# The first layer's experts in tiles of 32 columns, with a fixed order on the tensor engine and one block of whole-array matmuls per pair of experts

## The chip, the cores and the metric

The kernel runs on one core of a Trainium2 chip, all in fp32. The metric is the time of one execution on the device in microseconds (us), as the median of the runs shown. TensorE is PE below, its weight loads PEld, VectorE DVE, ScalarE ACT, GpSimd POOL and the queue that starts the loads SP.

## The reference, cut to what matters

The program computes a two-layer block (a state-space mixer, then experts; attention, then experts) on 512 rows of 1024 features and a context of 256 rows, and then a second block. The change lies in the experts of the first layer, which run twice: for the 512 rows of `x` (64 rows an expert) and for the 256 rows of the context (32 rows an expert). The 16 experts' weights are the same for both sets.

```python
N_EXPERTS, EC_CAPACITY, D_EXPERT = 16, 2, 1024
def moe_ec(h, router_w, w1, w3, w2):
    ...
    cap = EC_CAPACITY * T // N_EXPERTS          # 64 for x, 32 for the context
    aff = jax.nn.softmax(logits, axis=-1)
    gate, idx = lax.top_k(jnp.swapaxes(aff, 1, 2), cap)
    xg = h[bidx, idx]
    a = jnp.einsum('becd,edf->becf', xg, w1)
    g = jnp.einsum('becd,edf->becf', xg, w3)
    y = jnp.einsum('becf,efd->becd', jax.nn.silu(a) * g, w2)
    y = y * gate[..., None].astype(y.dtype)
    return jnp.zeros_like(h).at[bidx, idx].add(y.astype(h.dtype))
...
x = x + g2l * moe_ec(rmsnorm(x, norm2_w[i]) * (1.0 + sc2l) + sh2l, ...)
ctx = ctx + g2c * moe_ec(rmsnorm(ctx, norm2_w[i]) * (1.0 + sc2c) + sh2c, ...)
```

## The kernel before, in words

`Kern.moe` (L1073) goes over eight pairs of experts. For each pair there are three products, with w1, w3 (both in `moe_up`, L1151) and w2 (in `moe_down`, L1196). Here the gathered rows are the stationary operand (the weights of the array, in PE's sense) and the experts' weight matrices stream through as the moving one, 512 columns at a time. A product has eight K tiles of 128 features, so the stage has 8 pairs x 3 products x 8 = 192 K tiles. `moe_product` (L1132) issues for each K tile:

- the big set (L1142): for each half of the columns and each of the two experts a matmul whose stationary operand has 64 columns (the expert's 64 rows); the two experts take columns 0 to 63 and 64 to 127 of the array by `tile_position=(0, 64 * e)`. Results are `pa`, `pg` or `py`.
- the small set (L1148): for each expert and each half a matmul with 32 stationary columns; the four take the four quarters of the array's columns. Results are `ca`, `cg` or `cy`.

An fp32 matmul of this kind is two passes on PE, each with its own load, so the profile lists 8 passes of the big set and 8 of the small one for each K tile. The word **step** below means one pass of all tiles that share the array's columns: two passes side by side for tiles of 64 columns, four for tiles of 32.

The weights come through `Ring` (L106): nine tiles of 1 MiB, each two K tiles of one expert, loaded by SP (L125, L130) as the places come free. Around the products stand matmuls that use the whole array: `Router.quad` (L328) gathers the rows of four experts by a product with one-hot matrices (L343, 64 passes for each quad, results `xxg`; evicted by ACT at L347 and DVE at L349), `gates` (L351) does 16 small ones (L360), `flip` in `moe_up` transposes the activations (L1179, results `aT` and `cT`, evicted by ACT and DVE), and `moe_down` puts the results back: `scaled` multiplies by the gate and splits into `yhi` and `ylo` (L1226 ACT, L1227 DVE), `slots` makes one-hots `ohT` from a small matmul `sp` (L1233, L1237 DVE), and `scatter` multiplies the two (L1244, L1245, result `sc`) and adds it to the residual in SBUF (L1246, DVE; `xT` is the big set's residual, the `cT` with 128x256 elements the small one's). `after` (L1063) puts the gates of the first quad after pair 0's products with w1 and w3, and a gather with its gates after those of pairs 1, 3 and 5.

Nobody writes down the order of the engines: a scheduler merges the program's parts, by what is ready, into one list for each engine. PSUM is dealt out by `Slots` (L93), a table of banks by tag; the tags of this stage are `a`, `g`, `c` and `x`, two banks each.

Of the kernel before, what the change touches and what calls it, by code (L numbers as in the profile page):

```python
# [13 lines left out]
F32 = mybir.dt.float32  # L14
F32R = mybir.dt.float32r
# [7 lines left out]
P = 128  # L23
D = 1024
KT = 8
# [7 lines left out]
# columns of the packed per-feature vectors: (name, number of 128-tiles)  # L33
# [14 lines left out]
class SumSq:  # L48
    """Squares of [128, n] tiles summed tile by tile; the last ones stay apart until the sum over partitions."""
# [43 lines left out]
class Slots:  # L93
    """all of PSUM, bank by bank; the banks of a tag take turns"""
    MAP = dict(mm=(0, 1, 2), ada=(3,), aux=(4, 5), y=(6, 7), a=(0, 1), g=(2, 3), c=(4, 5), x=(6, 7), am=(0, 1, 4, 5), rms=(2, 3), vps=(6, 7))
# [39 lines left out]
class Head:  # L135
    """the second block's beginning: its h, as the residual becomes final, and the first products' part of the features that come early"""
# [25 lines left out]
    def begin(self, wp, pp):  # L162
        """products of the first four K tiles"""
# [22 lines left out]
class Pre:  # L186
    """hi + lo = x * gain of tokens a..b, with the sums of squares of x; 1/rms comes in at the end of the products."""
# [21 lines left out]
class Router:  # L209
    """Expert choice of the rows h = x * rs * A + sh of one set of tokens; residual tiles are fed as they become final."""  # L210

    def __init__(self, K, layer, xp, res, n, cap, c, nm):
# [28 lines left out]
    def score(self, k):  # L241
        """tile k's part of the logits and of the squares"""
# [19 lines left out]
    def turn(self, q):  # L262
        """tiles 4q..4q+3, times 1/rms, as rows"""
# [11 lines left out]
    def finish(self):  # L275
# [30 lines left out]
        # the cap largest of every expert (equal ones: the first), numbered from 1 by their place; 0: not taken  # L306
# [21 lines left out]
    def quad(self, q, pp, *tags):  # L328
        """gathered rows of 256 slots, transposed: xg[d, (expert, slot)]"""
# [21 lines left out]
    def gates(self, q, pp, tag):  # L351
        """the gates of the rows of the last quad"""
        K, nc, nt, cap, ne, oh = self.K, self.K.nc, self.nt, self.cap, self.ne, self.oh
        # gates: all experts' affinities of every slot, then the slot's own
# [6 lines left out]
        if cap == 32:  # L361
            # every row twice: for the two halves of the products' rows
# [15 lines left out]
class Kern:  # L378
# [24 lines left out]
    def consts(self):  # L403
# [18 lines left out]
        # silu of the conditioning, padded to a 32-column stationary operand  # L422
# [15 lines left out]
    def split(self, pool, raw, n=1024, eng=None):  # L438
        """raw (f32) = hi + lo, both exact in float32r."""
# [7 lines left out]
    def jobs(self, wp, jobs, look=1):  # L447
        """jobs: (weights or None, work). Weights are made ready some jobs ahead of their work; the background goes on after each product."""
# [28 lines left out]
    def dense(self, wp, pp, srcs, nk, act, rngs, evac, tag="mm", cols=P):  # L477
        """out^T tiles: srcs[i] holds [128, nk*cols] (pieces of <=1024 columns) of one tile of cols columns."""
# [24 lines left out]
    def rms(self, tp, pp, tiles, n, dim, tag="aux", rs=None, eng=None):  # L503
        """1/sqrt(mean of squares + eps) of the features in tiles (list of [128, n]), on all partitions."""
# [5 lines left out]
    def rs_of(self, tp, ps, n, dim, rs=None, after=None):  # L510
        """1/sqrt(ps / dim + eps); after: the activation that the table set for it may follow"""
# [8 lines left out]
    def table(self, after):  # L520
        """loads the table set that has both Ln and Exp; what is in the context comes after that"""
# [7 lines left out]
    # ------------------------------------------------------------------ modulation  # L529
# [4 lines left out]
    def ada_steps(self, tp, pp, layer, grp, tag, ttag="aux"):  # L534
        """one third of a layer's modulation, K tile by K tile"""
# [24 lines left out]
    def ada_half(self, tp, pp, hf):  # L560
        """shift and scale before the first mixer, of one half of the features"""
# [28 lines left out]
    def modulated(self, tp, src, rs, n, A, sh, hi, lo, f32=None, ks=range(KT)):  # L590
        """h = src * rs * A + sh, split to hi + lo (and kept whole in f32 if asked)."""
# [11 lines left out]
    # ------------------------------------------------------------------ layer 0: SSD mixer  # L603
    def ssd(self, e0, esc, rest):
        """The whole mixer of layer 0. e0: lives until the layer's end; esc: holds the context's residual; rest(cT): opens what follows,
        gives xT and the routers."""
# [5 lines left out]
        with ExitStack() as so:  # L612
# [6 lines left out]
            # triangles: tle[s, l] = s <= l, tge[s, l] = s >= l  # L619
# [40 lines left out]
            # the last scans run beside the context's output projection  # L660
# [23 lines left out]
            # fills the tensor engine's time until the choice is made  # L684
# [11 lines left out]
    def ssd_dt(self, tp, wp, pp, h, K, aS):  # L696
        """time steps, their running sums in each chunk (forward and backward heads) and decays"""
# [3 lines left out]
        # work in tiles of the first group, which come later  # L701
# [44 lines left out]
    def log1p(self, u, w, m, l):  # L746
        """u <- log(1 + u), accurate for small u (u >= 0)."""
# [11 lines left out]
    def ssd_in(self, g, wp, gp, pp, h, K, between):  # L759
        """convolved B, C, x and the gate 2*silu(z) of a group; tokens: latent, then context"""  # L760
# [7 lines left out]
        if g == 0:  # L768
            # as h comes
# [48 lines left out]
    def ssd_group(self, g, gp, pp, K, conv, zs):  # L818
        """the scans of a group, in twelve steps for the tensor engine to take between projections"""
# [36 lines left out]
        def prepare(c):  # L856
# [4 lines left out]
            # the smaller one of the two directions' exponents is the one that applies: forward for l > s, backward for l < s, 0 for l = s  # L861
# [102 lines left out]
    def ssd_proj(self, tp, yp, wp, pp, a, b, res, c, eng):  # L964
        """residual += gate * (gated norm of y) @ out_w for tokens a..b; yields after every K tile (None) and final tile (its number)"""
# [6 lines left out]
        for hf in range(2 // per):  # L972
# [33 lines left out]
            # the last two K tiles bank by bank, so that the banks get free one after the other  # L1006
# [28 lines left out]
        # slot number (from 1) of a partition: p % 64 + 1; for the halved set p % 32 + 1 in one half of every 64, none in the other  # L1035
# [12 lines left out]
        # fold[32 j + e, e'] = (e == e')  # L1048
# [3 lines left out]
        # twice[32 e + j, 64 e + 32 h + j] = 1  # L1052
# [10 lines left out]
    def after(self, r, pr, pp):  # L1063
        """what comes after the first products of a pair"""
# [8 lines left out]
    def moe(self, st, layer, R, nw2):  # L1073
        """R: routers of the sets (the first one with 64 slots an expert, the second one with 32)"""
# [1278 lines left out]
```

## Time and profile before

| | us |
|---|---|
| median of three runs | 3469.9 (3468.0 to 3475.1) |
| span of the profiled execution | 3464.9 |
| busy in the span: PE / PEld / DVE / ACT / POOL | 3278.8 / 2045.4 / 1667.4 / 1139.2 / 926.2 |
| the first layer's experts, from the end of the first quad's gather to the end of the last product | 941.8 to 1660.4 |
| from there to the first matmul of attention's projections | 1660.4 to 1679.9 |

The profile is one execution; the median of the runs lies 5.0 us above its span, and a predicted time below is a predicted span plus that. A busy share is time with any instruction in work. Matmuls overlap in the records, so what a step takes is read from the distance between the starts of records and not from their lengths. In a timeline a row can stand for several records ("x8"), with the start of the first; "128*64 128x512" is 128 rows by 64 stationary columns, moving operand 128x512.

### The profile page before, as it was taken

How to read it: one execution, taken by the hardware profiler on the slowest of the kernel's cores; microseconds unless marked ns; L12 is line 12 of the kernel's file. 1: busy time of each engine (PE TensorE's matmuls, PEld its weight loads, DVE VectorE, ACT ScalarE, POOL GpSimd, SP SyncE). 2: the span in 40 equal slices, each digit the busy share in tenths (PEclk: the TensorE clock that was granted, in tenths of full speed). 3: DMA queues.
4: the chain of work that ended last, by engine and by line, in shares of the span. 5: the costliest groups of instructions: out<-in, count | busy, mean ns of one | idle time of the engine just before them, and what ended most of it. 6: DMA issues, size and time to landing. Idle time of an engine off the chain costs nothing.

```text
span 3464.9 us, 44645 instructions
## 1 busy us (share of the span) xinstructions
PE 3278.8 (95%) x17408; PEld 2045.4 (59%) x17408; DVE 1667.4 (48%) x3070; ACT 1139.2 (33%) x2007; POOL 926.2 (27%) x638
## 2 busy tenths in 40 slices
PE   7999999989999999999899989998998999999998
PEld 4677777777623232322566754432356777888886
DVE  5588888886411111211456531003349954773322
ACT  4344444455300000000556520000135344573222
POOL 1344555543100000000341120000135454126543
PEclk9999999999999999999999999999999999999999
DMA  6454433454487767687234269999861322543232
GB/s 242 140 163 156 131 90 100 133 165 150 165 311 267 292 245 297 238 305 262 92 125 137 90 262 405 409 409 362 323 234 49 98 74 84 181 140 116 97 95 82
DMA packets 254083, 668.40 MB, mean 193 GB/s; under 512 B 19312, under 2 KB 73456, under 8 KB 252848
## 3 DMA queue, kind: packets, MB, share of 16 engines
q1 hardware_dynamic: 243920, 645.42, 52.1%
q10 hardware_dynamic: 9952, 20.12, 1.7%
q8 instruction: 137, 2.24, 0.3%
q14 instruction: 74, 0.61, 0.1%
HBM read 651.65 MB, written 13.83 MB: 192 GB/s over the span
## 4 chain that ended last, share of the span: by engine, by line
PE 60%; DVE 7%; DMA 4%; ACT 2%; issue 2%; POOL 1%; SPq 0%; DVEq 0%; POOLq 0%; ACTq 0%
PE pa L1142 7%; PE mm L473 6%; PE mm L475 6%; PE mm L474 6%; PE pg L1142 5%; PE py L1142 4%; PE py L1220 3%; DMA wm<-in_moe_w_dram 3%; PE ca L1148 2%; PE cg L1148 2%; PE gth L343 2%; PE cy L1148 2%; PE sc L1244 1%; PE pv L1436 1%; PE ptp L1427 1%
## 5 line engine op out<-in xcount | busy, mean ns | idle before, releaser
L444 POOL TENSOR_TENSOR wlo<-raw,whi 128x1024 fp32r<-128x1024 f32 (+3 forms) x207 | 461.4, 2231 | 1372.9 <-ACT whi L443 1339.4
L443 ACT CAST whi<-raw 128x1024 fp32r<-128x1024 f32 (+2 forms) x291 | 285.8, 984 | 486.6 <-PE mm L474 207.7
L473 PE MATMUL mm<-stk,whi 128*128 128x512 f32 (+2 forms) x944 | 342.8, 363 | 0.5 <-DVE pt__23035 L1581 0.5
L475 PE MATMUL mm<-stk,wlo 128*128 128x512 f32 (+2 forms) x944 | 336.1, 356 | 0.0
L474 PE MATMUL mm<-stk,whi 128*128 128x512 f32 (+2 forms) x944 | 335.4, 355 | 0.0
L1174 DVE TENSOR_TENSOR ac<-ac,pg 128x512 f32<-128x512 f32 x32 | 22.0, 687 | 531.5 <-PE pg L1142 531.0
L473 PE MATMUL pin<-hhi,whi 128*128 128x256 f32 (+1 forms) x768 | 271.5, 354 | 3.8 <-DVE acc L811 3.8
L475 PE MATMUL pin<-hhi,wlo 128*128 128x256 f32 (+1 forms) x768 | 265.5, 346 | 0.0
L474 PE MATMUL pin<-hlo,whi 128*128 128x256 f32 (+1 forms) x768 | 263.3, 343 | 0.0
L1142 PE MATMUL pa<-wm,xxg 128*64 128x512 f32 x760 | 223.6, 603 | 3.3 <-DMA wm<-in_moe_w_dram 2.8
L1142 PE MATMUL pg<-wm,xxg 128*64 128x512 f32 x712 | 209.4, 601 | 5.1 <-DMA wm<-in_moe_w_dram 5.1
L473 PEld LDWEIGHTS mm<-stk,whi 128*128 128x128 f32 (+1 forms) x944 | 180.3, 191 | 32.9 <-issue 7.9
L474 PEld LDWEIGHTS mm<-stk,whi 128*128 128x128 f32 (+1 forms) x944 | 180.0, 191 | 29.7 <-issue 5.9
L475 PEld LDWEIGHTS mm<-stk,wlo 128*128 128x128 f32 (+1 forms) x944 | 179.3, 190 | 25.9 <-issue 1.1
L58 POOL TENSOR_TENSOR sqa<-sqa,sq 128x256 f32<-128x256 f32 (+1 forms) x56 | 64.2, 1146 | 466.5 <-DVE acc L204 410.0
L473 PEld LDWEIGHTS pin<-hhi,whi 128*128 128x128 f32 x768 | 146.4, 191 | 45.0 <-issue 19.2
L474 PEld LDWEIGHTS pin<-hlo,whi 128*128 128x128 f32 x768 | 146.7, 191 | 19.6 <-DVE hlo L600 2.5
L475 PEld LDWEIGHTS pin<-hhi,wlo 128*128 128x128 f32 x768 | 146.4, 191 | 18.4 <-issue 1.7
L811 DVE SCALAR_TENSOR_TENSOR acc<-pin,cwh,acc 128x511 f32<-128x511 f32 (+3 forms) x256 | 148.5, 608 | 15.2 <-ACT acc L806 13.6
L1227 DVE SCALAR_TENSOR_TENSOR ylo<-py,xgate,yhi 128x512 fp32r<-128x512 f32 x32 | 24.0, 750 | 244.1 <-ACT yhi L1226 243.3
L1173 ACT ACTIVATE ac<-pa 128x512 f32<-128x512 f32 x32 | 19.0, 597 | 344.7 <-PE pa L1142 344.7
L1142 PEld LDWEIGHTS pg<-wm,xxg 128*64 128x64 f32 x712 | 59.1, 136 | 122.5 <-issue 95.4
(684 smaller groups left out, 7040.2 us busy)
## 6 DMA issues: line engine op xcount, KB each, us to landing
wm<-in_moe_w_dram SPq DMA_DIRECT2D x255, 1024.0 KB, 7.5
raw<-in_moe_w_dram SPq DMA_DIRECT2D x258, 512.0 KB, 6.9
raw<-in_ada_w_dram SPq DMA_DIRECT2D x96, 512.0 KB, 4.7
raw<-in_w_f_dram SPq DMA_DIRECT2D x68, 512.0 KB, 3.5
raw<-in_w_ssd_in_dram SPq DMA_DIRECT2D x48, 512.0 KB, 4.7
ab<-aS SPq DMA_DIRECT2D x96, 256.0 KB, 4.7
raw<-in_w_in_dram SPq DMA_DIRECT2D x33, 512.0 KB, 3.5
raw<-in_w_ssd_out_dram SPq DMA_DIRECT2D x32, 512.0 KB, 4.0
```

The costliest lines, as they stand in the source:

```text
L58: self.eng.tensor_tensor(self.acc, self.acc, self.late.popleft(), op=ALU.add)
L343: nc.tensor.matmul(ps[:, z2, :], r[:, t, k * P:(k + 1) * P], oh[:, t, :], start=(t == 0 and z == 0), stop=(t == nt - 1 and z == 1))
L443: nc.scalar.copy(hi[:, 0:n], raw[:, 0:n])
L444: (eng or self.lo).tensor_tensor(lo[:, 0:n], raw[:, 0:n], hi[:, 0:n].bitcast(F32), op=ALU.subtract)
L473: nc.tensor.matmul(ps, wh, ah, start=start, stop=False)
L474: nc.tensor.matmul(ps, wh, al, start=False, stop=False)
L475: nc.tensor.matmul(ps, wl, ah, start=False, stop=stop)
L811: nc.vector.scalar_tensor_tensor(o, p_[:, lo + s:hi + s], tap(j), o, op0=ALU.mult, op1=ALU.add)
L1142: nc.tensor.matmul(pb[hf][64 * e:64 * e + 64, :], lb(k, e), w[e][a][:, hf * 512:(hf + 1) * 512], tile_position=(0, 64 * e), **f)
L1148: nc.tensor.matmul(pc[o:o + 32, :], ls(k, e), w[e][a][:, hf * 512:(hf + 1) * 512], tile_position=(0, o), **f)
L1220: nc.tensor.matmul(py[half][64 * e:64 * e + 64, :], yb(k, e), w[e][a], start=(k == 0), stop=(k == KT - 1), tile_position=(0, 64 * e))
L1244: nc.tensor.matmul(ps[:, 0:n], y[0][:, kk * P:(kk + 1) * P], o, start=True, stop=False)
```

## The change

The first layer's `moe` no longer calls `moe_up` and `moe_down`. It has its own code (the second layer's `moe_last` keeps the old one), inside a block in which PE's order is the written one; the other engines are still scheduled.

```diff
-            after = self.after(R[0], pr, pp)
-            acts = self.moe_up(layer, pr, R, ring, ep, pp, after)
-            self.moe_down(layer, pr, R, ring, ep, pp, acts)
+        def product(nm, pr, lb, ls, pb, pc):
+            for q in range(4):
+                w = [ring.tile(...) for e in range(2)]
+                steps = [(a, z) for a in range(2) for z in (0, 1, 2)] if q < 3 else [(a, z) for z in (0, 1, 2) for a in range(2)]
+                for a, z in steps:
...
+                    for e in range(2):
+                        for h in range(2):
+                            o = 64 * e + 32 * h
+                            if z < 2:
+                                nc.tensor.matmul(pb[z][o:o + 32, :], lb(k, e)[:, 32 * h:32 * h + 32], w[e][a][:, z * 512:(z + 1) * 512], tile_position=(0, o), **f)
+                            else:
+                                nc.tensor.matmul(pc[o:o + 32, :], ls(k, e), w[e][a][:, h * 512:(h + 1) * 512], tile_position=(0, o), **f)
...
+        def scatter_small(y, o, k, kk):
+            ps = bank("scs", "s")
+            for j in range(2):
+                for z in range(2):
+                    nc.tensor.matmul(ps[:, j * C:(j + 1) * C], y[z][:, (kk + j) * P:(kk + j + 1) * P], o, start=j == 0 and z == 0, stop=j == 1 and z == 1)
+            for j in range(2):
+                t = ep.tile([P, C], F32, name="scc", tag="scc", bufs=2)
+                nc.scalar.activation(t, ps[:, j * C:(j + 1) * C], AF.Copy, scale=self.mod(layer, 5, 1, k + j))
+                nc.gpsimd.tensor_tensor(small.res[:, k + j, :], small.res[:, k + j, :], t, op=ALU.add)
...
+        with tc.manual_schedule(engines={mybir.EngineType.PE}):
+            big.quad(0, pp, "x", "c")
+            big.gates(0, pp, "x")
+            last = None
+            for pr in range(8):
+                product("moe_w1", ...)
+                ac = [silu(t) for t in (*pa, ca)]
+                product("moe_w3", ...)
+                for t, g in zip(ac, (*pg, cg)):
+                    nc.vector.tensor_tensor(t, t, g, op=ALU.mult)
+                for t, o in zip(ac, (aT[:, 0:4, :], aT[:, 4:8, :], cT)):
+                    flip(t, o)
+                if pr % 2 and pr < 7:
+                    big.quad(pr // 2 + 1, pp, "s")
+                    big.gates(pr // 2 + 1, pp, "s")
+                if last:
+                    scatter(*last)
+                product("moe_w2", ...)
+                last = (pr, [scaled(t, big.gate[:, pr:pr + 1]) for t in py], scaled(cy, small.gate[:, pr:pr + 1]))
+            scatter(*last)
```

In words:

- **Tiles.** The big set's matmul of 64 stationary columns becomes two of 32 (new L1101), so all products, the small set's (new L1103) too, go in quads of 32 columns. A K tile now has 16 passes of the big set and 8 of the small one, still six steps.
- **Order.** In the last quarter of each product the two K tiles of `pb[0]` come first, then those of `pb[1]`, then those of `pc`. All matmuls that use the whole array stand in one block for each pair, between the products with w3 and w2: 12 transposes, then for pairs 1, 3 and 5 a gather with its gates, then the scatter of the pair before (40 or so passes: `sp` twice, 16 `sc`, 16 `scs`). The last pair's scatter stands at the end. The gates of the first quad move ahead of pair 0.
- **Engines.** The big set's residual is still updated by DVE (new L1139). The small set's goes by a copy with scale on ACT (new L1148, `scc`) and an add on POOL (new L1149); before, both were DVE's.
- **Buffers.** A tag `s` of four PSUM banks (6, 0, 7, 1) serves the scatters and the later gathers; `ac`, `yhi` and `ylo` get a third buffer; the small one-hots get their own tag `ohS`. The silu of `pa` and `ca` is written ahead of the product with w3.

PE where pair 0's products end and pair 1's begin, in the kernel before (`sel` is a table for the one-hots, `xslotT` the slot numbers):

```order
L1142 MATMUL py<-wm,aT 64x512 x4
L1148 MATMUL cy<-wm,cT 32x512 x4
L1233 LDWEIGHTS sel
L1233 MATMUL sp<-xslotT,sel 128x512
L1142 MATMUL pa<-raw,xxg 64x512 x3
L1244 MATMUL sc<-ohT,yhi 128x512
L1245 MATMUL sc<-ohT,ylo 128x512
L1244 MATMUL sc<-ohT,yhi 128x512
L1245 MATMUL sc<-ohT,ylo 128x512
L1142 MATMUL pa<-raw,xxg 64x512
L1148 MATMUL ca<-raw,cxg 32x512
```

The scatter of pair 0 is spread in small pieces over the next pair's product with w1.

PE at the block of pair 2 in the changed kernel, from the end of the product with w3 to the start of that with w2 (`ident` is the identity matrix of the transposes, `ohS` the small set's one-hots):

```order
L1103 MATMUL cg<-raw,cxg 32x512 x2
L1103 MATMUL cg<-wm,cxg 32x512 x2
L1113 MATMUL tp<-ident,ac 128x128 x12
L1127 LDWEIGHTS sel
L1127 MATMUL sp<-xslotT,sel 128x512
L1127 LDWEIGHTS sel
L1127 MATMUL sp<-cslotT,sel 128x256
L1138 MATMUL sc<-ohT,yhi 128x512
...
L1145 MATMUL scs<-ohS,yhi 128x256
...
L1101 MATMUL py<-wm,aT 32x512 x8
L1103 MATMUL cy<-wm,cT 32x512 x4
```

No product matmul stands between the transposes and the last scatter any more; in the places marked "..." the sixteen `sc` and sixteen `scs` matmuls of pair 1 alternate, four and four.

POOL at the end of the stage, the difference (`wlo` is the low part of attention's weights, `kB` a buffer of attention that is cleared, `slots` the router's):

```order
 L325 TENSOR_TENSOR slots<-slots,wk 16x512
 L326 CAST xslotT<-slots 16x512
-L444 TENSOR_TENSOR wlo<-raw,whi 128x1024 x3
-L1311 MEMSET kB 64x3072
+L1149 TENSOR_TENSOR cT<-cT,scc 128x256 x56
+L444 TENSOR_TENSOR wlo<-raw,whi 128x1024 x2
+L1411 MEMSET kB 64x3072
+L1149 TENSOR_TENSOR cT<-cT,scc 128x256 x2
+L444 TENSOR_TENSOR wlo<-raw,whi 128x1024
+L1149 TENSOR_TENSOR cT<-cT,scc 128x256 x6
```

POOL had no work of this stage; it now has 64 adds, and the last eight stand behind two splits and the clearing, with a third split between them.

## Rows read from the trace of the kernel before

**Rows 1.** By stretch: span, busy PE to POOL, PE clock, DMA share, GB/s.
```profile
941.80:1660.40 718.60, 715.31 (x3664) 208.02 (x3662) 128.45 (x236) 46.05 (x85) 0.00 (x0) 1.00 0.74 278
994.50:997.90 3.40, 3.40 (x9) 0.95 (x6) 1.85 (x5) 0.35 (x2) 0.00 (x0) 0.51 1.02 419
1660.40:1679.90 19.50, 17.64 (x63) 9.95 (x59) 13.55 (x25) 13.27 (x21) 10.74 (x11) 0.91 0.25 84
2100.00:2300.00 200.00, 194.61 (x944) 86.17 (x941) 21.09 (x46) 16.36 (x32) 0.00 (x0) 1.00 1.03 409
```

**Rows 2.** Timeline, one K tile: start, length, engine, line, names, shapes, records.
```profile
965.44 1.94 PE L1142 MATMUL pa<-raw,xxg 128*64 128x512 f32 x8
967.31 1.07 PE L1148 MATMUL ca<-raw,cxg 128*32 128x512 f32 x8
968.30 0.64 PE L1142 MATMUL pg<-raw,xxg 128*64 128x512 f32 x1
```

**Rows 3.** Timeline, PE: four quads of 32 columns, two lone passes, what follows.
```profile
63.55 2.76 PE L542 MATMUL ada<-raw,sc 128*32 128x512 f32 x18
66.25 0.38 PE L473 MATMUL pin<-hhi,whi 128*128 128x256 f32 x1
```

**Rows 4.** Timeline, PE: pair 0's scatter between pair 1's first matmuls.
```profile
1020.73 1.93 PE L1142 MATMUL pa<-raw,xxg 128*64 128x512 f32 x6
1022.59 0.50 PE L1244 MATMUL sc<-ohT,yhi 128*128 128x512 f32 x1
...
1023.16 0.40 PE L1244 MATMUL sc<-ohT,yhi 128*128 128x512 f32 x1
1023.39 0.40 PE L1245 MATMUL sc<-ohT,ylo 128*128 128x512 f32 x1
1023.72 1.07 PE L1142 MATMUL pa<-raw,xxg 128*64 128x512 f32 x2
```

**Rows 5.** Timeline, PE: short passes of the scan, transposes, gathers.
```profile
731.53 0.61 PE L900 MATMUL y<-ce,hst 128*64 128x128 f32 x8
731.97 0.39 PE L900 MATMUL y<-w,rowx 128*64 128x128 f32 x4
...
993.02 1.28 PE L1179 MATMUL tp<-ident,ac 128*128 128x128 f32 x8
...
1085.75 0.28 PE L343 MATMUL gth<-xoh,xrh 128*128 128x256 f32 x1
1085.86 0.28 PE L343 MATMUL gth<-xoh,xrl 128*128 128x256 f32 x1
```

**Rows 6.** Groups by line and form, 930 to 1670: busy us, mean ns, idle before.
```profile
L1174 DVE TENSOR_TENSOR ac<-ac,cg 128x512 f32<-128x512 f32 x8 | 5.5, 684 | 0.4
L1181 DVE COPY aT<-tp 128x256 f32<-128x256 f32 x16 | 6.7, 421 | 5.5 <-ACT aT L1180 5.5
L1237 DVE TENSOR_SCALAR ohT<-sp,iop 128x512 fp32r<-128x512 f32 x8 | 5.9, 742 | 0.0
L1237 DVE TENSOR_SCALAR ohT<-sp,iop 128x256 fp32r<-128x256 f32 x14 | 6.1, 475 | 0.0
L1246 DVE SCALAR_TENSOR_TENSOR xT<-sc,mods,xT 128x512 f32<-128x512 f32 x63 | 45.2, 747 | 51.8 <-PE sc L1245 51.7
```

**Rows 7.** Groups, timeline, and the chain's last two lines: the stage's end.
```profile
L58 POOL TENSOR_TENSOR sqa<-sqa,sq 128x256 f32<-128x256 f32 x36 | 34.5, 957 | 27.1 <-ACT sq L65 26.4
...
1661.64 7.05 POOL L444 TENSOR_TENSOR wlo<-raw,whi 128x1024 fp32r<-128x1024 f32 x3 [739.90 <-ACT whi L443]
1672.43 2.66 POOL L1311 MEMSET kB<- 64x3072 f32 x1 [3.74 <-DVE ohT L1237]
...
L1266 ACT ACTIVATE sq<-xT 128x512 f32<-128x512 f32 x8 | 5.0, 631 | 4.6 <-PE rmsps L1268 4.6
...
1675.89 0.87 PE rmsps L1268 x2
...
1679.89 0.96 PE mm L473 x3
```

More of the change, by code (lines that the diff above doesn't have):

```diff
@@ L1073, in moe @@
     def moe(self, st, layer, R, nw2):
+        nc, tc = self.nc, self.tc
         ep = self.pool(st, "moe_e")
-        R[0].xgp = ep
+        big, small = R
+        big.xgp = ep
         rings, _ = self.wm1[:-1], self.wm1[-1]
         if nw2:
-            rings.append((st.enter_context(self.tc.tile_pool(name="moe_w2", bufs=nw2, side="right")), nw2))
+            rings.append((st.enter_context(tc.tile_pool(name="moe_w2", bufs=nw2, side="right")), nw2))
         ring = Ring(self, rings, 3)
-        pp = self.pp or self.pool(st, "moe_ps", bufs=2, space=PSUM)
@@ L1082, in moe @@
-        R[0].quad(0, pp, "x", "c")
-        for pr in range(8):
-            after = self.after(R[0], pr, pp)
-            acts = self.moe_up(layer, pr, R, ring, ep, pp, after)
-            self.moe_down(layer, pr, R, ring, ep, pp, acts)
+        pp = self.pp
+        sel, iop = self.mk["sel"], self.mk["iop"]
+        bank = lambda nm, tag: pp.tile([P, 512], F32, name=nm, tag=tag)
+        def product(nm, pr, lb, ls, pb, pc):
+            for q in range(4):
+                w = [ring.tile(self.I[nm][layer, 2 * pr + e, q * 256:(q + 1) * 256, :]) for e in range(2)]
+                steps = [(a, z) for a in range(2) for z in (0, 1, 2)] if q < 3 else [(a, z) for z in (0, 1, 2) for a in range(2)]
+                for a, z in steps:
+                    k = 2 * q + a
+                    f = dict(start=(k == 0), stop=(k == KT - 1))
+                    for e in range(2):
[5 more added lines that the diff above has]
+                                nc.tensor.matmul(pc[o:o + 32, :], ls(k, e), w[e][a][:, h * 512:(h + 1) * 512], tile_position=(0, o), **f)
@@ new lines, in silu, with flip @@
+        def silu(src):
+            t = ep.tile([P, 512], F32, name="ac", tag="ac", bufs=3)
+            nc.scalar.activation(t, src, AF.Silu)
+            return t
+        def flip(src, dst):
+            tp = bank("tp", "x")
+            for j in range(4):
+                nc.tensor.transpose(tp[:, j * P:(j + 1) * P], src[:, j * P:(j + 1) * P], self.ident)
+            nc.scalar.copy(dst[:, 0:2, :].rearrange("p a b -> p (a b)"), tp[:, 0:256])
+            nc.vector.tensor_copy(dst[:, 2:4, :].rearrange("p a b -> p (a b)"), tp[:, 256:512])
@@ new lines, in scaled, with slots @@
+        def scaled(src, gate):
+            hi = ep.tile([P, 512], F32R, name="yhi", tag="yhi", bufs=3)
+            lo = ep.tile([P, 512], F32R, name="ylo", tag="ylo", bufs=3)
+            nc.scalar.activation(hi, src, AF.Copy, scale=gate)
+            nc.vector.scalar_tensor_tensor(lo, src, gate, hi.bitcast(F32), op0=ALU.mult, op1=ALU.subtract)
+            return hi, lo
+        def slots(s, pr, cols):
+            n = s.n
+            ps = bank("sp", "s")
+            nc.tensor.matmul(ps[:, 0:n], sel[:, pr].rearrange("p e j -> p (e j)"), s.slotT, start=True, stop=True)
+            r = []
+            for cix in cols:
+                t = ep.tile([P, 512], F32R, name="ohT", tag="ohT", bufs=2)[:, 0:n] if n == S else ep.tile([P, C], F32R, name="ohS", tag="ohS", bufs=2)
+                nc.vector.tensor_scalar(t, ps[:, 0:n], iop[:, cix:cix + 1], None, op0=ALU.is_equal)
+                r.append(t)
+            return r
@@ new lines, in scatter_big @@
+        def scatter_big(y, o, k, kk):
+            ps = bank("sc", "s")
+            for z in range(2):
+                nc.tensor.matmul(ps, y[z][:, kk * P:(kk + 1) * P], o, start=(z == 0), stop=(z == 1))
+            nc.vector.scalar_tensor_tensor(big.res[:, k, :], ps, self.mod(layer, 5, 0, k), big.res[:, k, :], op0=ALU.mult, op1=ALU.add)
+        def scatter_small(y, o, k, kk):
+            ps = bank("scs", "s")
+            for j in range(2):
+                for z in range(2):
+                    nc.tensor.matmul(ps[:, j * C:(j + 1) * C], y[z][:, (kk + j) * P:(kk + j + 1) * P], o, start=(j == 0 and z == 0), stop=(j == 1 and z == 1))
+            for j in range(2):
+                t = ep.tile([P, C], F32, name="scc", tag="scc", bufs=2)
+                nc.scalar.activation(t, ps[:, j * C:(j + 1) * C], AF.Copy, scale=self.mod(layer, 5, 1, k + j))
+                nc.gpsimd.tensor_tensor(small.res[:, k + j, :], small.res[:, k + j, :], t, op=ALU.add)
```

19 lines of the change are left out of this document (18 added, 1 removed).

## The prediction

> **What bounds the kernel now.** The table by stretch comes first, because the share of busy time says little: PE is busy in 715.3 of the 718.6 us of the first layer's experts, at a granted clock of 1.00, with DMA at 278 GB/s and a share of 0.74 [rows 1]. So the stage is PE's, the weights arrive in time, and the question is what PE does in it. The timeline of one K tile answers most: the big set's part starts at 965.44, the small one's at 967.31, the next K tile at 968.30 [rows 2]. That is 2.86 us for six steps. Four steps and a change of tile width take 1.87, two steps and a change 0.99, so a step is about 0.44 and a change about 0.11. The two quads, two lone passes and the exit that the next view shows take 66.25 - 63.55 = 2.70 us for six steps [rows 3]; it has 16 passes in four quads and then two single ones. With two steps and a change at 0.99 this gives 0.43 for the step and 0.13 for the exit. I take 0.43 for a step and 0.14 for a change.
>
> The third view is the scatter's stretch [rows 4]. There x6 passes hold two full and two lone steps and cost 1.86 us like four full ones, and the x2 behind the scatter cost as much as two full steps: a pair that is broken up pays for its idle half, and each return to the whole array pays an exit again. The stage has 192 x 2.86 = 549.1 us in whole K tiles; the other 169.5 us are whole-array work, such exits, lone steps and waits.
>
> **The change part by part.**
>
> *Products.* All six steps of a K tile now have the same tile width, so both changes go: 6 x 0.43 = 2.58 us, and 192 x 2.58 = 495.4. That is 53.7 us less. The doubling of the big set's passes costs no step, if four tiles of 32 columns run abreast as the four in [rows 3] and the small set's in [rows 2] do.
>
> *Whole-array work.* It replaces the 169.5 us. Prices of its pieces: a scatter pass of 512 columns 0.23 (1023.39 less 1023.16) [rows 4]; a transpose 1.28/8 = 0.16, a gather pass 0.11 to 0.12, both [rows 5]; DVE's part from [rows 6]. A short block (pairs 2, 4, 6, 7) has 12 transposes (1.9), 16 `sc` (3.7), 16 `scs` at a gather pass's price (1.9) and two `sp` (0.5): 8.0 us of PE. DVE's path is longer: last multiply 0.68, two copies of `aT` 0.84, a wait for `sp` of about two of its passes, 0.4, one-hots 0.74, copy of `cT` 0.42, two small one-hots 0.95, then residual updates at 0.75. The last `scs` (the twelfth result in four banks) needs the bank of the eighth, which is the sixth `sc`: 6 x 0.75 = 4.5. Then four passes, 0.5, and handovers between engines, which I put at 0.8. That makes 9.8 us. The handovers are the least certain; at nothing and at double they move seven blocks by 5.6 us either way. A long block (pairs 1, 3, 5) has a gather (64 x 0.12 = 7.7) and 16 gate passes at 0.11, taken like the gather's (1.8), besides, less the 0.4 of waiting for `sp` that they cover: 18.9. Pair 0's block has only the multiply, the last four transposes and a copy, 0.68 + 0.64 + 0.42 and the same 0.8: 2.5. The first quad's gates, 1.8 and the 0.5 of an eviction, are 2.3 ahead of pair 0. Sum: 2.3 + 2.5 + 3 x 18.9 + 4 x 9.8 = 100.7, against 169.5.
>
> *The clock.* Behind a group of gates and transposes with gaps the granted clock was 0.51 (its lower level, 1.2 GHz) for 3.4 us, 994.5 to 997.9, while PE was busy in all of it [rows 1]; this cost 1.7 us, and came once for four groups of gates. Seven blocks of whole-array passes with DVE in the way offer seven such places. I take one in two, 6 us; ends: none, and twice the length at each, 24.
>
> *Engines that take over work.* POOL gets eight adds of 0.96 for a pair [rows 7], 7.7 us in a time of at least 70, behind ACT copies; with two `scc` buffers the third add waits, but the `scs` results they free are not the ones that the last passes wait for. Inside the stage this costs nothing: what follows a block on PE is the product with w2, which needs none of it. If the cover were gone, the excess over the block would be a few us a pair.
>
> *The stage.* 495.4 + 100.7 + 6 = 602.1, so 116.5 us less than 718.6.
>
> *The tail.* Here the change loses. Before, 19.5 us lie between the stage's end and attention's first matmul [rows 1], and POOL's splits and clearing run beside DVE's scatter. Now POOL's order is two splits, the clearing, two adds, one split, six adds. The first split starts some 2.0 us after the last product (ACT has a third `yhi` before its cast); then 2 x 2.35 + 2.66 + 2 x 0.96 + 2.35 + 6 x 0.96 = 17.4 [rows 7], so the last add ends at 19.4. ACT's first square reuses a buffer that waits for that add, so behind it come one square (0.63), eight sums of 0.86 (6.9) and the 3.1 us from the last sum's end (1675.89 + 0.87) to the first matmul at 1679.89 [rows 7]: 29.8 in all. Loss 10.3. If the squares did not wait for POOL, the scatter on PE and DVE would end near 10 and the loss would be about 0; if the adds took half as long again as in [rows 7], 14. Both go into the range.
>
> *Sum.* -116.5 + 10.3 = -106.2. The span goes from 3464.9 to 3358.7; with the 5.0 by which the median lies over the profiled span, **3364 us**.
>
> **The rivals.**
>
> *A step never settles (a).* If the quad's step stays at 0.45, a little over the 0.44 that [rows 2] alone give, 1152 steps x 0.02 = 23 us come back: 3387. Against it stands the settled 0.43 of [rows 3].
>
> *Issue (b).* A step now needs four loads and four matmuls, 8 instructions in 0.43 us, 54 ns each; before, a pair needed four. In a run of gathers one instruction takes 1085.86 - 1085.75 = 0.11, halved 55 to 60 ns [rows 5]. If that is PE's rate of issue and not of work, a step becomes 8 x 59 ns = 0.47 and 1152 x 0.04 = 48 us are lost: 3412. Against it: 8 passes and their 8 loads from 731.53 to 731.97, 0.44 us or 27 ns each [rows 5]. So a small chance.
>
> *Weights (c).* In products one round of four tiles' loads (2 MiB) is used in 5.16 us, 406 GB/s, about the most that the trace shows over 200 us (409) [rows 1]; the nine tiles in hand and the blocks between bring the need to 718.6 x 278 / 602 = 332 on average. If only 320 arrived, the stage would take 624 us: 3386.
>
> *Slower (d).* Two of a quad's four tiles now read the same weight rows at the same time; in [rows 2] and [rows 3] all four read different ones. If such tiles ran one after the other, the big set's 768 steps would take twice their time, 330 us more: 3694. The point at which the change loses is a mean step of 0.43 + 106.2 / 1152 = 0.522 us. Against it: each tile has its own moving operand anyway, and four of those keep to 0.43 in [rows 3].
>
> *Slower, in part (f).* The four tiles could overlap incompletely once quads follow each other for 20 us, which no row shows: the longest run is four quads [rows 3]. The step would then lie between 0.43 and the 0.86 of (d); a third more, 0.57, would cost 1152 x 0.14 = 161 us: 3525. Against it: inside [rows 3] six steps and the exit leave no room for such a step. The Trainium skill, "TensorE: Matmul & The Clock Gate", section "Measured speedup vs the span model", gives a measured gain of 3.07 for four row tiles and 2.38 for three column tiles where full overlap would give 4 and 3. By that a step would be 0.43 x 4 / 3.07 = 0.56 and the time 3514, an estimate from that page; the 2.70 us of [rows 3] do not agree with it.
>
> *Not what it says (e).* The fixed order takes away the scheduler's fillers: where DVE is late nothing else runs. If each of seven blocks took 15 us more, the gain would be gone. The scheduler's order, though, paid lone steps and exits in 169.5 us for work that needs some 90.
>
> **How the numbers follow.** The forecast has 0.76; (a) 0.07, (b) 0.06, (c) 0.05, (d) 0.02, (f) 0.02, (e) 0.02. The forecast's own range comes from its bounds: no clock loss and no handovers give -6 - 5.6, the tail without its loss -10.3, which do not come together: 3346; clock 18 and handovers 5.6 more, tail 4 more give 3392. This takes in (a) and (c). With (b), (d), (e) and (f) outside, and something for costs not thought of, about 0.85 lies within 3346 to 3394. About 0.2% (7 us) is what a measurement of this kernel can tell from no change. All cases but (d), (e) and (f) are faster: 0.94; (e) may end within 0.2%: same 0.01; slower 0.05.
>
> **What would show it.** Right: 2.58 us from K tile to K tile, quads of four records with starts some 0.43 apart; blocks of some 10 and 19 us between the products with w3 and w2, in which PE waits for DVE's `xT` and one-hots; the stage near 602 us; the gap to attention's first matmul near 30, with POOL's last `cT` add ahead of the first square. Wrong: steps of 0.47 or above with PEld "issue" (b), waits for `wm` and `raw` inside products (c), quads whose records start 0.2 or more apart (d), steps of 0.5 or more with the four starts together (f), blocks over 25 us (e).

## The result and the profile after

The changed kernel takes 3372.3 us (median of 4 runs, 3370.8 to 3374.8) against 3472.5 us before: a ratio of 0.9711 with a 95% interval of 0.9697 to 0.9725, faster by 2.9%. The prediction was 3364 us, with a range of 3346 to 3394. The profiled execution has a span of 3373.1 us, 91.8 less than before; its own time lies 1.7 above its span.

The table by stretch, core 0, as in [rows 1]: the stage from the end of the first quad's gather to the end of the last product, the blocks of pairs 1, 3 and 4, and the tail, from the last product to attention's first matmul.

```profile
944.55:1556.50 611.95, 592.75 (x5201) 230.39 (x5200) 107.84 (x180) 73.38 (x141) 40.46 (x56) 0.99 0.84 326
1051.77:1078.10 26.33, 21.51 (x131) 18.64 (x127) 11.13 (x21) 6.02 (x13) 3.55 (x5) 0.87 0.34 134
1211.30:1235.04 23.74, 19.84 (x130) 17.31 (x126) 11.11 (x21) 6.01 (x13) 3.51 (x5) 0.93 0.39 157
1297.00:1306.60 9.60, 8.05 (x50) 6.38 (x46) 8.42 (x15) 3.86 (x9) 3.58 (x6) 1.00 0.88 346
1556.50:1588.40 31.90, 20.54 (x62) 10.64 (x58) 9.28 (x15) 16.56 (x29) 16.26 (x19) 0.79 0.21 66
```

The stage went from 718.6 to 612.0 us, and the tail from 19.5 to 31.9. The first quad's gather, ahead of the stage, took 11.7 us instead of 9.8. PE now stands still for 19.2 us in the stage, where it stood for 3.3, and the blocks with a gather have a granted clock below 1.

The timeline of PE in one K tile, as in [rows 2]:

```profile
1000.16 1.90 PE L1101 MATMUL py<-wm,aT 128*32 128x512 f32 x16
1001.87 1.04 PE L1103 MATMUL cy<-wm,cT 128*32 128x512 f32 x8
1002.73 1.04 PE L1101 MATMUL py<-wm,aT 128*32 128x512 f32 x8
```

1002.73 - 1000.16 = 2.57 us for six steps where [rows 2] have 2.86: 0.43 a step, no change of width. All 24 products take 20.6 to 20.7 us from their first matmul to what follows, 48 steps of 0.43.

The timeline of the gather in pair 3's block, at one of its four stops:

```profile
1214.19 0.28 PE L343 MATMUL gth<-xoh,xrl 128*128 128x256 f32 x1
1214.51 0.54 DVE L349 TENSOR_SCALAR xxg<-gth,A,mods 128x256 f32<-128x256 f32 x1
1215.11 0.39 PE L343 MATMUL gth<-xoh,xrh 128*128 128x256 f32 x1 [0.64 <-DVE xxg L349]
```

A bank holds two K tiles of gathered rows. The code writes the first half, evicts it by DVE, then writes the second half, and PE waits for that eviction before it starts the second: 0.92 us from start to start where 0.12 is usual, four times a gather. Before, the scheduler ran passes of another bank while DVE evicted, so that the wait hardly showed. The timeline of the first gather in the kernel before:

```profile
933.72 0.54 DVE L349 TENSOR_SCALAR xxg<-gth,A,mods 128x256 f32<-128x256 f32 x1 [11.03 <-PE gth L343]
933.80 0.28 PE L343 MATMUL gth<-xoh,xrl 128*128 128x256 f32 x1
...
934.04 0.28 PE L343 MATMUL gth<-xoh,xrl 128*128 128x256 f32 x1
934.32 0.38 PE L343 MATMUL gth<-xoh,xrh 128*128 128x256 f32 x1
```

The step there is 0.28 us (934.04 to 934.32). In the changed kernel the groups of PE over the whole execution have the stops in sum, and with them what the scatters wait for:

```profile
L343 PE MATMUL gth<-xoh,xrh 128*128 128x256 f32 x128 | 34.9, 307 | 11.2 <-DVE xxg L349 10.3 <-DVE cT L1115 0.9
...
L1138 PE MATMUL sc<-ohT,yhi 128*128 128x512 f32 x64 | 29.2, 456 | 10.5 <-ACT scc L1148 5.2 <-DVE ohT L1131 4.2 <-DVE cT L1115 1.1
```

The timeline of the tail, by engine (POOL, then ACT and PE), has the order that the prediction went by:

```profile
1558.32 4.75 POOL L444 TENSOR_TENSOR wlo<-raw,whi 128x1024 fp32r<-128x1024 f32 x2 [20.43 <-ACT whi L443]
1563.14 2.65 POOL L1411 MEMSET kB<- 64x3072 f32 x1
1565.87 1.40 POOL L1149 TENSOR_TENSOR cT<-cT,scc 128x256 f32<-128x256 f32 x2
1567.23 2.36 POOL L444 TENSOR_TENSOR wlo<-raw,whi 128x1024 fp32r<-128x1024 f32 x1
1569.55 4.13 POOL L1149 TENSOR_TENSOR cT<-cT,scc 128x256 f32<-128x256 f32 x6
...
1566.62 0.47 ACT L1148 ACTIVATE scc<-scs,mods 128x256 f32<-128x256 f32 x1 [5.75 <-POOL cT L1149]
1567.83 0.80 PE L1138 MATMUL sc<-ohT,yhi 128*128 128x512 f32 x1 [5.23 <-ACT scc L1148]
1573.72 0.63 ACT L1366 ACTIVATE sq<-xT 128x512 f32<-128x512 f32 x1 [0.89 <-POOL cT L1149]
1574.40 8.94 PE L1368 MATMUL rmsps<-sq,ones 128*128 128x512 f32 x14 [3.64 <-ACT sq L1366]
1588.43 0.73 PE L473 MATMUL mm<-hhi,whi 128*128 128x512 f32 x2
```

The last add ends at 1573.68, 17.2 us after the last product; ACT's first square follows at once. Ahead of it PE waits 5.23 us for a copy on ACT, which waits for POOL. From the end of that wait to 1579 the granted clock is 0.50, the lower level of 1.2 GHz (the table by stretch):

```profile
1567.80:1579.00 11.20, 7.53 (x14) 4.17 (x15) 1.65 (x3) 4.30 (x8) 6.92 (x14) 0.50 0.30 94
```

### The profile page after: what moved, and what is told of

Its sections match the earlier page's. It is cut to its first block, busy times and chain, and to the rows that moved or that the text cites. A ratio compares the mean times of both kernels' runs of the same rounds, so it can differ in the third digit from the quotient of the medians.

```text
span 3373.1 us, 47879 instructions
## 1 busy us (share of the span) xinstructions
PE 3160.7 (94%) x18944; PEld 2070.1 (61%) x18944; DVE 1642.3 (49%) x3006; ACT 1169.9 (35%) x2071; POOL 971.8 (29%) x702
## 4 chain that ended last, share of the span: by engine, by line
PE 58%; DVE 8%; DMA 4%; ACT 2%; issue 2%; POOL 1%; SPq 0%; DVEq 0%; POOLq 0%; ACTq 0%
PE mm L473 6%; PE mm L475 6%; PE mm L474 6%; PE py L1320 3%; PE py L1101 3%; PE pa L1101 3%; PE pg L1101 3%; DMA wm<-in_moe_w_dram 3%; PE pa L1242 2%; PE gth L343 2%; PE pg L1242 2%; PE cy L1103 2%; PE ca L1103 2%; PE cg L1103 2%; PE pv L1536 1%
## 5 line engine op out<-in xcount | busy, mean ns | idle before, releaser
L1149 POOL TENSOR_TENSOR cT<-cT,scc 128x256 f32<-128x256 f32 x64 | 46.0, 748 | 575.0 <-ACT scc L1148 574.6
L865 DVE SCALAR_TENSOR_TENSOR m<-ab,acum,m 128x128 f32<-128x128 f32 x192 | 118.2, 658 | 23.7 <-POOL m L863 23.7
L444 DVE TENSOR_TENSOR wlo<-raw,whi 128x1024 fp32r<-128x1024 f32 (+1 forms) x84 | 104.7, 1250 | 47.4 <-ACT whi L443 46.6
L1242 PE MATMUL pa<-wm,xxg 128*64 128x512 f32 x416 | 112.6, 597 | 1.9 <-DMA wm<-in_moe_w_dram 1.9
```

Of the source, the lines that this page charges most:

```text
L444: (eng or self.lo).tensor_tensor(lo[:, 0:n], raw[:, 0:n], hi[:, 0:n].bitcast(F32), op=ALU.subtract)
L865: nc.vector.scalar_tensor_tensor(m[:, r, :], ab[:, r, :], acum[:, c, 4 * g + r:4 * g + r + 1], m[:, r, :], op0=ALU.subtract, op1=ALU.min)
L1242: nc.tensor.matmul(pb[hf][64 * e:64 * e + 64, :], lb(k, e), w[e][a][:, hf * 512:(hf + 1) * 512], tile_position=(0, 64 * e), **f)
```

## The experiments

The result agrees with the prediction, but not yet with its reasons: it gave 54 us to the tiles and the rest of the stage's gain to the order. The first runs part the two. Times below are medians, and ratios are to the kernel before in the same set of runs; block and gather lengths are from the start of one matmul to the start of the first one behind.

**Order without tiles (e1_wide).**

```diff
-                        for h in range(2):
-                            o = 64 * e + 32 * h
-                            if z < 2:
-                                nc.tensor.matmul(pb[z][o:o + 32, :], lb(k, e)[:, 32 * h:32 * h + 32], ...)
+                        if z < 2:
+                            nc.tensor.matmul(pb[z][64 * e:64 * e + 64, :], lb(k, e), ..., tile_position=(0, 64 * e), **f)
```

> The changed kernel with the big set's matmuls back at 64 columns, the fixed order kept. Theory (the change of tile width is paid at every return, 0.14 us each way): 7 of 8 K tiles of a product change width twice, 24 x 7 x 0.28 = 47 us come back, the product takes 22.6 us instead of 20.62, and the time is some 3419 us. Rival (in a fixed order without scatter pieces between them the change of width costs less, and the gain came from the order): 3372 to 3385 us, product at 20.7 to 21.

3425.2 us, ratio 0.9871 (0.9857 to 0.9886). The timeline of PE in one K tile shows [rows 2] again:

```profile
1000.53 1.94 PE L1099 MATMUL py<-raw,aT 128*64 128x512 f32 x8
1002.40 1.06 PE L1103 MATMUL cy<-raw,cT 128*32 128x512 f32 x8
1003.39 1.08 PE L1099 MATMUL py<-wm,aT 128*64 128x512 f32 x4
```

2.86 us, and each product 22.6. The theory holds: a change of width costs the same with nothing between the products. Added up from the starts of the records, the products take 542.9 us instead of 495.6, the 47 us expected. The median moved by more, some 53 us (3425.2 - 3372.3; 55 by the ratios): in the traces the blocks of pairs 2, 4, 6 and 7, which the edit doesn't touch, take 10.7 to 11.3 us instead of 9.3 to 9.8, together 5.7 more, at a granted clock of 0.84 to 0.85 instead of 1.00.

**Tiles without anything else (e7_tiles).** The kernel before, with the first layer's big set in four tiles of 32 columns:

```diff
+                        if pc is not None:
+                            for h in range(2):
+                                o = 64 * e + 32 * h
+                                nc.tensor.matmul(pb[hf][o:o + 32, :], lb(k, e)[:, 32 * h:32 * h + 32], ..., tile_position=(0, o), **f)
+                            continue
```

> The kernel before with one edit, the first layer's big set in tiles of 32 columns; scheduler, banks and scatter as they were. Theory (the width changes are worth 54 us wherever they go): 3472 - 54 = 3418 us. Rival (the scheduler's pieces cut quads, 72 of them, and each cut costs two steps, 0.86 us, where a cut pair cost the same or nothing): up to 30 us less gain, 3430 to 3450 us.

3381.4 us, ratio 0.9742 (0.9720 to 0.9764): 88 us, more than either theory. Both traces have the same 88 exits from column tiles in the stage and the same scatter passes; the starts of the records add up to 92.0 us less in the products (521.6 instead of 613.6) and to the same, within 0.2 us, for every kind of whole-array work in the stage. Whole K tiles explain 54 of it: beyond them the products spent 613.6 - 549.1 = 64.5 us before, and spend 521.6 - 495.4 = 26.2 now. The timeline of PE at pair 0's scatter, the same place as [rows 4], shows the rest:

```profile
1015.66 1.90 PE L1145 MATMUL pa<-raw,xxg 128*32 128x512 f32 x10
1017.49 0.50 PE L1250 MATMUL sc<-ohT,yhi 128*128 128x512 f32 x1
...
1018.62 0.63 PE L1145 MATMUL pa<-raw,xxg 128*32 128x512 f32 x3
1018.64 0.62 PE L1154 MATMUL ca<-raw,cxg 128*32 128x512 f32 x1
1019.08 0.61 PE L1145 MATMUL pa<-raw,xxg 128*32 128x512 f32 x3
1019.10 0.59 PE L1154 MATMUL ca<-raw,cxg 128*32 128x512 f32 x1
1019.62 0.50 PE L1250 MATMUL sc<-ohT,yhi 128*128 128x512 f32 x1
```

The scatter cuts a quad, but the three left-over passes of `pa` start together with one of `ca`: tiles of one width and of four different columns run abreast whatever product they belong to. This piece of four matmuls takes 1.00 us. The same place before has one `pa` of 64 columns and one `ca` of 32, which did not share a step: about 1.0 us for the first alone [rows 4], and as much for the second, which the timeline has next; the whole array is back at 1025.70:

```profile
1024.72 1.05 PE L1148 MATMUL ca<-raw,cxg 128*32 128x512 f32 x2
```

So one width removes not only the changes but most of the lost steps: of 64.5 us for lost steps and exits, 26.2 are left.

**The whole change without the fixed order (e2_sched).**

```diff
-        with tc.manual_schedule(engines={mybir.EngineType.PE}):
+        if True:
```

> The changed kernel, all in tiles of 32 columns, with PE's order given back to the scheduler. Theory A (the order is worth what the tiles don't explain, 106.7 - 54 = 53 us of the stage): some 3425 us. Theory B (the blocks' waits cost about as much as the broken quads did; the scheduler's list has 33 returns to the whole array and 22 broken quads against 8 and 0, that is 22 x 2 x 0.43 + 25 x 0.14 = 22 us more, but it fills the waits of the blocks, some 30 us): 3360 to 3385 us.

3369.6 us, ratio 0.9709 (0.9694 to 0.9723), the same as the change. Theory A falls. From first to last product it takes 608.7 us where the changed kernel takes 610.2, and PE is never idle. Theory B holds in its parts too: by the starts of the records the products take 516.0 us instead of 495.6, so cuts and exits cost 20.4 (B has 22), and from the first gather to the last product everything else takes 102.2 instead of 128.0, so 25.8 of waits are filled (B has some 30). A cut costs its steps at the cut, and behind it nothing more is lost. The timeline of PE in pair 0's product with w2, behind one:

```profile
1010.87 0.59 PE L1103 MATMUL cy<-wm,cT 128*32 128x512 f32 x1
1011.28 0.60 PE L1101 MATMUL py<-wm,aT 128*32 128x512 f32 x3
1011.30 1.87 PE L1103 MATMUL cy<-wm,cT 128*32 128x512 f32 x12
1012.59 0.59 PE L1101 MATMUL pa<-raw,xxg 128*32 128x512 f32 x1
1013.00 0.60 PE L1103 MATMUL cy<-wm,cT 128*32 128x512 f32 x3
```

Quads go on one tile out of phase, three of one result and one of the next, at the full step (1013.00 - 1011.28 is four times 0.43).

**The gather's halves together (e3_gather).** Both halves of a bank are written, then evicted:

```diff
-                                         start=(t == 0 and z == 0), stop=(t == nt - 1 and z == 1))
+                                         start=(t == 0 and z == 0 and not (both and z2)), stop=(t == nt - 1 and z == 1 and not (both and z2 == 0)))
+                if both and z2 == 0:
+                    continue
...
```

> The changed kernel with the two halves of each gather bank written one behind the other and evicted after both, so that the second half does not wait for the first half's eviction. Theory (in the fixed order that wait of 0.92 us stands four times in each of four gathers and nothing fills it): the gathers fall from 11.3 to 7.7 us, 4 x 3.6 = 14.4 us less, some 3358 us; if the lower clock behind the gathers came from these gaps, up to 4 us more. Rival (the wait moves to the one-hots or the gates behind the gather): under 5 us, 3368 us or more.

3368.3 us, ratio 0.9701 (0.9682 to 0.9720); its runs spread from 3356 to 3371. The gathers take 7.8 us (8.1 for the first), the wait for `xxg` is gone from the group's row, and from the first gather to the last product it is 609.0 us instead of 623.6: 14.6 less, where 14.4 were expected. Of these 7.7 arrive in the span: behind the stage this execution spent 4.1 us more, which nothing in the edit explains, and its first gather began 2.9 us later. The median, 4 us below the change, leaves open how much of the 14 is kept; e6_both bears on it.

```profile
L343 PE MATMUL gth<-xoh,xrh 128*128 128x256 f32 x128 | 31.5, 288 | 0.9 <-DVE cT L1119 0.9
```

The lower clock stayed in two of the three blocks (0.92), so the gather's stops were not its only cause. In the changed kernel's own trace, too, pair 3's block has a granted clock of 1.00 up to its gates and 0.70 only behind them, from the wait for the one-hots into the scatter (1226.4 to 1232.0).

**The last pair's small set on DVE (e4_tail).**

```diff
+                if dve:
+                    nc.vector.scalar_tensor_tensor(small.res[:, k + j, :], ps[:, j * C:(j + 1) * C], self.mod(layer, 5, 1, k + j), small.res[:, k + j, :], op0=ALU.mult, op1=ALU.add)
+                    continue
...
-            scatter(*last)
+            scatter(*last, dve=True)
```

> The changed kernel with the last pair's small set added by DVE, as before, instead of ACT and POOL. Theory (the 31.9 us between the last product and attention's first matmul are long because eight adds stand behind two splits and the clearing on POOL, and ACT's first square waits for the last of them): the gap falls to some 21 us, 3361 us. Rival (the gap is long because the scatter on PE no longer overlaps the sums of squares): 30 us or more, 3370 us.

3366.1 us, ratio 0.9697 (0.9680 to 0.9713). The tail is 21.5 us, as the theory has it. The timeline of ACT and PE there:

```profile
1569.87 0.63 ACT L1369 ACTIVATE sq<-xT 128x512 f32<-128x512 f32 x1 [5.44 <-PE scs L1145]
...
1570.55 6.66 PE L1371 MATMUL rmsps<-sq,ones 128*128 128x512 f32 x14 [0.86 <-ACT sq L1369]
...
1582.30 0.73 PE L473 MATMUL mm<-hhi,whi 128*128 128x512 f32 x2
```

The last product ended at 1560.78. The squares now start after 9.1 us instead of 17.2, although POOL's splits and clearing still run until 1572.5. The granted clock is 1.00 in the whole tail. The median fell by 6.2 us and not by the tail's 10.4; in this trace the first gather, ahead of the edit, began 5.5 us later.

**All of the small set on DVE (e5_dve).** The same lines for every pair.

> The changed kernel with all of the small set's adds on DVE, none on ACT and POOL. Theory (DVE's path sets the blocks; the bank that the last scs waits for then stands behind four more updates of 0.48): each of seven blocks grows by 1.9 us, 13 us, and the tail falls by 10: some 3375 us. Rival (PE sets the blocks, DVE has room): only the tail's 10 us, 3362 us.

3370.0 us, ratio 0.9714 (0.9695 to 0.9734), between the theories. The tail is 21.4 us, and the blocks of pairs 2, 4, 6 and 7 take 10.75, 11.72, 12.05 and 11.47 us instead of 9.32, 9.64, 9.82 and 9.84: 1.8 more on average. Not all of that is DVE's. The table by stretch of pair 2's and pair 4's blocks here, and of pair 2's in e6_both, where DVE has no more work in a block than in the change:

```profile
1137.32:1148.07 10.75, 9.39 (x50) 6.07 (x47) 9.61 (x20) 1.12 (x3) 0.00 (x0) 1.00 0.82 327
1296.90:1308.62 11.72, 10.12 (x50) 7.49 (x46) 9.93 (x20) 1.12 (x3) 0.00 (x0) 0.85 0.77 305
...
1138.23:1148.99 10.76, 9.54 (x50) 7.58 (x46) 8.53 (x15) 3.74 (x9) 3.52 (x5) 0.84 0.83 333
```

The lower clock alone makes a short block 1.4 us longer (10.76 against 9.32). Of the short blocks only pair 2's ran at 1.00 here as in the change, and DVE's added updates cost it 1.4 us. The waits in pair 2's block, in the change and here:

```profile
PEld scs L1145 <- DVE xT L1139: 0.2, 1, 0.2
...
PEld scs L1145 <- DVE xT L1139: 1.0, 3, 0.4
```

So DVE's updates set the end of a block once the small set is among them; in the change, without it, they hardly hold PE. The move to ACT and POOL gains 8.7 us over the seven blocks of these two traces, the lower clock's share included, and loses 10.5 in the tail.

**Both repairs (e6_both), and one-hots ahead of the block (e8_hots).** The second adds to the first:

```diff
+                if last:
+                    last = (hots(pr - 1), *last[1:])
                 pg, cg = [bank("pg", "g") for _ in range(2)], bank("cg", "c")
                 product("moe_w3", ...)
```

where `hots` is the old `slots` for both sets, with its `sp` in the banks of tag `x`. The last pair's own one-hots are made at the end of its block.

> The gather's halves written together and the last pair's small set on DVE. Theory (two separate waits, one in the blocks, one behind the stage): the gains add, 12.8 us as measured in the gather's run between first and last product and 10.5 for the tail, some 3349 us. Rival (a gain in one is given back in the other): 3356 us or more.

> As the run with both, and the one-hots of a pair made between the next pair's products with w1 and w3 instead of inside the block. Theory (in the block DVE has 1.7 us of one-hots and PE waits for the first of them): seven blocks are shorter by 1.3 to 1.7 us each, less 0.6 for each new return to the whole array, net 5 to 8 us, 3342 us. Rival (the updates that follow set the block's end, and the matmuls for the one-hots break the products): 3349 us or more.

3349.0 us, ratio 0.9650 (0.9634 to 0.9666), and 3342.1 us, ratio 0.9634 (0.9618 to 0.9651). Both times come out as the theory says. Against e4_tail, measured beside it, the gather's edit in e6_both is worth 17.1 us by the medians and 9.6 from the first gather to the last product in the traces; the lower clock in the blocks of pairs 1 and 2 (0.85 and 0.84) took part of the 14 there. With the one-hots early, the scatter's row and the table by stretch (the blocks of pairs 1 and 3, and the tail) are:

```profile
L1142 PE MATMUL sc<-ohT,yhi 128*128 128x512 f32 x64 | 26.9, 420 | 1.9 <-DVE cT L1119 1.8
```

```profile
1056.20:1074.90 18.70, 17.30 (x132) 15.65 (x132) 9.89 (x19) 6.08 (x13) 3.59 (x6) 1.00 0.45 174
1208.40:1225.90 17.50, 17.02 (x132) 15.64 (x132) 9.90 (x19) 6.09 (x13) 3.60 (x6) 1.00 0.49 193
1541.10:1561.70 20.60, 17.17 (x61) 8.49 (x57) 10.75 (x21) 13.02 (x21) 10.72 (x11) 1.00 0.33 103
```

The long blocks take 18.6 and 17.4 us, and the granted clock is 1.00 in all three stretches; from the end of the first gather to the last product it is 594.3 us instead of e6_both's 604.8. The gain does not lie where the theory put it, evenly in seven blocks: against blocks at full clock, the short ones of pairs 2 and 4 lost only 0.7 and 0.6 us, pair 6's 1.9, and pair 7's grew by 0.4; the long ones of pairs 3 and 5 lost 2.8, about half of it the clock's.

**The best version, with the scheduler's order and again with the fixed one (e9_free, e10_again).** The same one-line edit as in e2_sched.

> The version with early one-hots, PE's order given back to the scheduler. Its list has 24 returns to the whole array and 9 broken quads, against 15 and none with the fixed order: 9 x 0.86 + 9 x 0.14 = 9 us more; what it can fill are the waits left in the blocks, 1 to 2 us in each of seven. Theory (the order by itself is worth about nothing either way): within 7 us of the version with the fixed order, 3338 to 3350 us. Rival (once the fixed order's waits are gone it is worth 10 us or more): 3352 to 3365 us.

> The version with early one-hots again, on the same chip as the one with the scheduler's order, for the comparison: 3342 us; all theories.

3343.5 us, ratio 0.9641 (0.9624 to 0.9657), and 3345.8 us, ratio 0.9648 (0.9634 to 0.9661). The order by itself is worth nothing here either. The version with early one-hots is the fastest that was run, with either order: 3.5 to 3.7% below the kernel before and, by the ratios, some 25 us below the change. The times alone do not part its second measurement from e6_both (0.9648 and 0.9650); the traces do, 594.7 us in the stage against 604.8.

## Why the prediction was right or wrong

- **Products: right.** 192 x 2.58 = 495.4 us were forecast; 24 products of 20.6 to 20.7 make 495 to 497. Rivals (a), (b), (d) and (f), which all raise the step, are out by the K tile of 2.57 us: four tiles run abreast for 20 us on end, two of them on the same weight rows. From the speed-up that it quoted from the Trainium skill ("TensorE: Matmul & The Clock Gate", section "Measured speedup vs the span model") the prediction estimated a step of 0.56; here the measurement decides, it is 0.43.
- **Weights (c): not seen.** DMA moved 326 GB/s over the stage, close to the 332 worked out, and no product took longer than 20.7 us.
- **Short blocks: right in length, not in path.** 9.3 to 9.8 us against 9.8. The forecast let PE wait at the end for DVE's sixth residual update. In the trace the waits for `xT` come to 0.6 us in all seven blocks, and only at PE's loads: from the first `sc` on the 32 passes run through in 5.9 us, and the 3.4 to 3.9 us ahead of it are transposes, `sp` and waits for DVE's copies and one-hots. That the two paths are equally long is luck; they are close, as e5_dve shows, where a few more updates make DVE's the longer.
- **Long blocks: wrong.** 18.9 us were forecast, 26.3, 23.7 and 23.7 measured. The step that failed is the gather's "64 x 0.12 = 7.7": it took the price of a pass from rows in which a scheduler fills the stops, and gave it to an order in which nothing can. The wait was in the code of `quad`, half for half. It adds 3.6 us to a gather of 7.7 and so 10.8 in the stage; the first gather, which the forecast left as it was, takes 1.9 more than before. e3_gather takes the wait away.
- **The clock: about right in size, not in place.** 6 us were forecast. From the first `sc` to the block's end the long blocks take 7.3, 7.3 and 7.2 us where the short ones, at 1.00, take 5.9; and pair 1's gather, with a granted clock of 0.59 from 1058 to 1061, takes 12.7 where the other two take 11.3. That is 4.0 + 1.4 = 5.4 us. It came to the long blocks alone, not to one in two of seven, and e1_wide, e5_dve and e6_both have it in short blocks too.
- **The tail: right in its chain, two terms off in opposite directions.** 29.8 us forecast (its terms add up to 30.0), 31.9 measured. An add on POOL took 0.69 us (4.13 / 6), not the 0.96 of [rows 7], so the last add came at 17.2 instead of 19.4; but from the first square to attention's first matmul it took 14.7 instead of 10.6. That the two nearly cancel is luck. e4_tail shows the chain: without the adds on POOL the squares start 8.1 us earlier, and what follows them takes 12.4, at a granted clock of 1.00. So the 5.2 us stop with the lower clock behind it cost 2.3 of the 4.1; the rest is left in e4_tail too, where a table load of 1.28 us on ACT stands between two squares, and the forecast left that out.
- **The sum.** 14.4 us of span are missing (91.8 against 106.2): 9.9 in the stage, 2.1 in the tail, 1.9 in the first gather, the rest ahead of it and behind the tail. By the medians the error is smaller, 8 us: the change's profiled execution was the slowest of its four, so its median lies 0.8 below its span and not 5.0 above. That too is luck.
- **Its reasons: wrong in one point.** The prediction priced the tiles at 53.7 us and let 100.7 us of blocks replace 169.5 of whole-array work, exits, lone steps and waits. The two add up only one way round: with wide tiles all the rest of the change is worth 44 us, the tail's loss included (e1_wide), and the tiles behind it some 53. But by e7_tiles the tiles alone bring 88 us in the old structure, and all the rest then brings some 9 more (3381.4 to 3372.3, intervals that overlap): tiles and blocks remove in large part the same loss. By e2_sched and e9_free PE's fixed order by itself adds nothing once the tiles have one width; with wide tiles it was not run apart from the rest. Rival (e), that the order takes the scheduler's fillers away, was right as a mechanism: 19.2 us of standing still, about the 20.4 that cuts and exits cost in e2_sched. Its sign, a block over 25 us, came once, in pair 1.

## What to carry to other kernels

Where small matmuls share the array, give all of them one tile width: here a change of width cost a quarter of a step or more each way (0.11 to 0.14 of 0.43 us), and tiles of one width filled each other's gaps across products, even after a cut. Before an order is written out by hand, look for waits inside each helper that the scheduler had filled from elsewhere, above all two halves of a bank written and read in turn. And when work moves to an idle engine, read what that engine has queued at the end of the stage: there the last items decide.

## What the runs showed of the hardware

- Column tiles of 32 that belong to different accumulations start within 20 ns of each other and share a step (1018.62 and 1018.64 in e7_tiles), and quads that are out of phase with the program go on at 0.43 us a step (1011.28 to 1013.00 in e2_sched).
- The granted clock of TensorE fell to 0.50 (its lower level, 1.2 GHz) in the tail behind PE's 5.2 us stop; with that stop gone (e4_tail) the tail ran at 1.00 (its higher level, 2.4 GHz). In the long blocks it fell to means of 0.87 and 0.93, in pair 3's only behind a wait for one-hots; with the one-hots early the same blocks ran at 1.00 (e8_hots), with the gather's stops alone removed two of three did not (e3_gather, 0.92). The wait for one-hots is not all of it: pair 2's short block has it in the change, at 1.00, and in e6_both, at 0.84. What else decides stays open.
